# A hybrid decoder layer on one core: the embedding's product by input block, and a fixed order for the last instructions

## The chip, the core and the metric

The kernel runs on one NeuronCore of a Trainium2 chip. Five engines work side by side, each with a queue of its own that it takes strictly in order: TensorE (PE in the profile, with its weight loads as PEld), VectorE (DVE), ScalarE (ACT), GpSimd (POOL) and SyncE (SP), which here only issues transfers. Engines wait for each other through semaphores. Sixteen DMA engines move data between HBM and the on-chip memory SBUF; matmul results go to PSUM, eight banks of 128 x 512 fp32. The metric is the device time of one execution in microseconds, the median of several runs.

## The reference

One decoder layer on 512 tokens of width 1024, in fp32: an FFN, a token mixer, a second FFN, then a gated embedding and a last RMSNorm. Only the last part is touched by the change:

```python
h = h + 0.5 * swiglu(rmsnorm(h, ffn1_norm), ...)
...
h = h + 0.5 * swiglu(rmsnorm(h, ffn2_norm), ...)
gate = sigmoid(rmsnorm(h, ple_norm) @ ple_w_gate + ple_b_gate)
h = h + gate * (p @ ple_w_proj)          # p is (512, 256), ple_w_proj (256, 1024)
return rmsnorm(h, final_norm)
```

The product `p @ ple_w_proj` depends on no other layer's result, so the kernel computes it first of all and stores it in HBM; "the embedding" below is this product.

## The kernel before

**Numbers as pairs.** Every fp32 operand of a product is split into a rounded high part (ACT's cast, `whi`, line 532) and a low part (DVE's difference, `wlo`, line 536). A product is three matmuls: high x high, high x low, low x high. Activations lie feature-major: a tile `h[d]` has 128 features on the partitions and 512 tokens along the free axis; weights are the stationary operand.

**Steps.** The layer up to the second FFN is a list of steps. Each has a load (SP), a split (ACT and DVE), a product (PE) and what comes after the product. Steps 0 and 1 are the embedding, steps 2 to 5 the first block of the FFN in its plain form, from step 6 on a group of seven products of quarter blocks follows for each further block (a Strassen scheme), among them steps with weights that are sums of two loads: POOL issues accumulating loads for these (lines 761 and 764), or DVE adds (`sums`, line 756). Early steps also have the forms of x among their split work: h is scaled and cast (lines 630 and 634), its low parts taken (637), and differences of token halves and feature halves formed (646, 680, 682). Those are the names `split1.1`, `split3.1`, `split4.1`, `split4.2`, `split5.2`, `split5.3` and `split6.2` in the order.

**An order written out by hand.** `run` makes a task of each of these works and then takes them in the order of the text `ENTRY`. `split3.1:4` means the next four instructions of that task, `split3.1` all that is left of it. Within `tc.manual_schedule(engines=ORDERED)` PE, ACT, DVE and SP keep the program's order; POOL is free. Behind that block (the gates and the last norm) a list scheduler orders the instructions by priority and by a model of their times.

**The embedding.** Step q computes four of the eight 128-feature outputs from both input blocks k of p. Step 0's order is k, then pass, then output; step 1's is output first. Step 0 accumulates in three `sm` banks and one `acc` bank, step 1 in three `mm` banks and one `acc` bank. Loads: `p[:, 0]`, step 0's weights in three parts, `p[:, 1]`, then step 1's weights in one transfer and the table of vectors, then the slices of x. `out` (line 1065) copies the four results to SBUF, two on ACT and two on DVE, and `store_embedding` sends them to HBM.

**The tail.** The gates of blocks 0 to 4 are taken for all 512 tokens at a time; those of blocks 5, 6 and 7 by token halves, first half a (tokens 0 to 255) of all three, then half b. `gate` is: a product with r (DVE, 1742), the sigmoid (ACT, 1743), the product with the embedding (DVE, 1744), the sum into h (DVE, 1745), the square (ACT, 1748, or DVE, 1750, for block 7). POOL adds the squares of blocks 0 to 6 into `total` (1769, 1789); `gained` scales h by the last norm's gain. `factors` sums `total` and block 7's square over the features with four small matmuls against a column of ones (1799) and takes the inverse root, for half a by DVE alone (eleven small instructions), for half b with ACT's square root. `rows_out` transposes each chunk of 128 tokens back to rows by PE (1809), two groups of four tiles a chunk, scales one group on ACT (1812) and one on DVE (1814) and stores them (1815). In the program `factors` of half a stands between blocks 6 and 7 of half b, and `rows_out` behind all gates; where they run among the others the scheduler decides.

## Time and profile before

| | us |
|---|---|
| median of three runs | 1072.11 (1071.75 to 1072.2) |
| the profiled execution | 1071.36 |
| its span, first to last instruction | 1069.6 |
| PE busy in the span | 1059.4 |
| DVE, ACT, POOL busy | 781.0, 513.8, 135.5 |

A row of the timeline has the start, the duration, the engine, the line, the operation, the output and inputs by their names in the program, shapes and a count where like instructions are merged, and in brackets how long the engine had been idle and what released it. A row of a table of stretches has each engine's busy time with the count of instructions, the granted clock of TensorE, the mean share of the DMA engines in use and what they moved in GB/s. The chain of waits gives start, length and what the end hung on. The last instruction of the span is not the last computation: the scalings of the last rows begin at 1064.5, and the rest is their way to HBM.

### The profile page before, as it was taken

What the parts mean: (1) busy time and instruction counts of PE and PEld (TensorE: products, weight loads), DVE (VectorE), ACT (ScalarE), POOL (GpSimd) and SP (SyncE); (2) the same over time, 40 slices, a digit from 0 to 9 for tenths busy, and PEclk for the clock granted to TensorE, in tenths of its full rate; (3) what the DMA queues carried; (4) which work ended last, traced back from release to release, by engine and by line L of the source; (5) the groups of instructions that cost most, each with busy time, mean ns of one, the idle gap of its engine ahead of it and who ended that gap; (6) DMA issues with size and microseconds to landing.
All of it is one profiled execution on the core that took longest, in us unless ns stands there. A gap on an engine that the chain in (4) does not pass through costs nothing.

```text
span 1069.6 us, 19076 instructions
## 1 busy us (share of the span) xinstructions
PE 1059.4 (99%) x7926; PEld 993.5 (93%) x7926; DVE 781.0 (73%) x1082; ACT 513.8 (48%) x716; POOL 135.5 (13%) x125
## 2 busy tenths in 40 slices
PE   9999999999999999999999999999999999999997
PEld 8999999999999898887888888999999999999996
DVE  7987676766667686776998756687766677667766
ACT  7644444344444364664753434354444434443554
POOL 0100000000000300034333000001100000000311
PEclk9999999999999999999999999999999999999998
DMA  9987766666523232543431323667766676634412
GB/s 343 307 229 195 190 189 186 162 179 173 138 60 119 71 110 90 154 142 119 154 102 62 105 90 118 214 176 201 197 143 188 162 198 182 187 105 115 142 41 79
DMA packets 50327, 163.70 MB, mean 153 GB/s; under 512 B 5696, under 2 KB 6208, under 8 KB 50240
## 3 DMA queue, kind: packets, MB, share of 16 engines
q1 hardware_dynamic: 40304, 128.86, 35.0%
q0 software_dynamic: 8640, 31.46, 16.9%
q10 hardware_dynamic: 1296, 2.16, 0.7%
q8 instruction: 62, 1.02, 0.4%
q14 instruction: 25, 0.20, 0.1%
HBM read 158.20 MB, written 4.26 MB: 152 GB/s over the span
## 4 chain that ended last, share of the span: by engine, by line
PE 96%; DVE 1%; ACT 1%; DMA 1%; SPq 0%; issue 0%; DVEq 0%; ACTq 0%
PE sm L248 25%; PE mm L746 20%; PE a L746 15%; PE mm L232 7%; PE sm L232 7%; PE mm L248 6%; PE a L232 4%; PE a L248 3%; PE sm L835 2%; PE mm L835 1%; PE a L835 1%; PE sm L301 1%; PE sm L1388 1%; DMA g<-in_p 1%; PE sm L1632 1%; PE sm L1452 0%
## 5 line engine op out<-in xcount | busy, mean ns | idle before, releaser
L532 ACT CAST whi<-raw 128x1024 fp32r<-128x1024 f32 (+1 forms) x140 | 144.4, 1032 | 152.1 <-issue 56.2
L536 DVE TENSOR_TENSOR wlo<-raw,whi 128x1024 fp32r<-128x1024 f32 (+1 forms) x140 | 172.7, 1234 | 60.5 <-ACT whi L532 57.5
L746 PE MATMUL mm<-xfb,whi 128*128 128x256 f32 x960 | 166.1, 276 | 0.0
L248 PE MATMUL sm<-glo,whix 128*128 128x256 f32 (+1 forms) x512 | 151.1, 295 | 0.0
L248 PE MATMUL sm<-ghi,wlox 128*128 128x256 f32 x592 | 150.8, 277 | 0.0
L248 PE MATMUL sm<-ghi,whix 128*128 128x256 f32 (+1 forms) x512 | 150.4, 294 | 0.0
L746 PEld LDWEIGHTS mm<-xfb,whi 128*128 128x128 f32 x960 | 144.5, 188 | 0.0
L746 PE MATMUL mm<-xfb,wlo 128*128 128x256 f32 x480 | 132.5, 276 | 0.0
L248 PEld LDWEIGHTS sm<-ghi,wlox 128*128 128x128 f32 x592 | 111.2, 188 | 6.8
L746 PE MATMUL a<-xfb,whi 128*128 128x256 f32 x640 | 110.8, 276 | 0.0
L746 PEld LDWEIGHTS a<-xfb,whi 128*128 128x128 f32 x640 | 96.3, 188 | 0.0
L248 PEld LDWEIGHTS sm<-ghi,whix 128*128 128x128 f32 x512 | 96.1, 188 | 0.0
L248 PEld LDWEIGHTS sm<-glo,whix 128*128 128x128 f32 x512 | 96.1, 188 | 0.0
L746 PEld LDWEIGHTS mm<-xfb,wlo 128*128 128x128 f32 x480 | 90.1, 188 | 0.0
L536 DVE TENSOR_TENSOR wlox<-rawd,whix 128x1024 fp32r<-128x1024 f32 (+1 forms) x40 | 45.6, 1141 | 60.1 <-ACT whix L532 60.1
L746 PE MATMUL a<-xfb,wlo 128*128 128x256 f32 x320 | 88.3, 276 | 0.0
L536 DVE TENSOR_TENSOR wlo<-rawb,whi 128x1024 fp32r<-128x1024 f32 x52 | 63.6, 1222 | 18.6 <-ACT whi L532 18.5
L895 ACT ACTIVATE g<-g 128x512 f32<-128x512 f32 x40 | 25.3, 632 | 105.4 <-DVE g L893 105.4
L761 POOL DMA_DIRECT2D raw<-in_ffn_gu x20 | 17.3, 865 | 427.1 <-DVE h L951 164.7
L232 PE MATMUL sm<-x,whi 128*128 128x512 f32 x224 | 71.0, 398 | 0.0
L532 ACT CAST whi<-rawb 128x1024 fp32r<-128x1024 f32 x52 | 54.3, 1045 | 27.3 <-DVE rawb L756 17.6
L951 DVE SCALAR_TENSOR_TENSOR h<-sm,h 128x512 f32<-128x512 f32 x96 | 63.5, 683 | 4.4 <-PE sm L248 4.2
(388 smaller groups left out, 2498.0 us busy)
## 6 DMA issues: line engine op xcount, KB each, us to landing
raw<-in_ffn_gu SPq DMA_DIRECT2D x56, 512.0 KB, 6.6
rawd<-in_ffn_down SPq DMA_DIRECT2D x40, 512.0 KB, 4.6
rawb<-in_ffn_gu SPq DMA_DIRECT2D x32, 512.0 KB, 6.1
raw<-in_ffn_gu POOLq DMA_DIRECT2D x30, 512.0 KB, 5.5
raw<-in_w_in SPq DMA_DIRECT2D x28, 512.0 KB, 3.8
s<-in_ffn_gu SPq DMA_DIRECT2D x20, 512.0 KB, 7.7
s<-in_ffn_gu POOLq DMA_DIRECT2D x20, 512.0 KB, 8.9
raw<-in_w_out SPq DMA_DIRECT2D x16, 512.0 KB, 3.4
```

What stands on the lines that cost most here:

```text
L232: nc.tensor.matmul(ps, w, x, start=first and n == 0, stop=last and n == 2, skip_group_check=True)
L248: nc.tensor.matmul(ps[:, tok], wt[:, c], xt[:, tok], start=first and k == i == 0, stop=last and k == len(xs) - 1 and i == len(by_part) - 1 ...
L301: nc.tensor.matmul(ps[:, c : c + 1], part[:, c * P : (c + 1) * P], ones[:, 0:1], start=part is t, stop=part is not t or more is None,)
L532: nc.scalar.copy(self.hi[:, c], self.raw[:, c])
L536: nc.vector.tensor_tensor(self.lo[:, c], self.raw[:, c], self.hi[:, c].bitcast(F32), ALU.subtract)
L746: nc.tensor.matmul(o, wt[:, c], xt, start=fresh and p == m == n == 0, stop=last and n == 2, skip_group_check=True,)
L761: nc.gpsimd.dma_start(w21.raw, self.src[0], accum_op=ALU.add)
L835: nc.tensor.matmul(by_half(ps)[:, s], (whi, whi, wlo)[n][:, c], t[:, s, n % 2], start=not lower and p == i == 0, stop=lower and p == len(s ...
L895: nc.scalar.activation(t, t, AF.Silu)
L951: nc.vector.scalar_tensor_tensor(h[d], ps[d], 0.5, h[d], ALU.mult, ALU.add)
L1388: nc.tensor.matmul(ps, chunk(b_tok[g], c), to_state[g][c], start=True, stop=True)
L1632: nc.tensor.matmul(chunk(ps, c), chunk(v[c][i // 4], i % 4), chunk(ws[i // 4], i % 4), start=True, stop=True,)
```

## The change

Three parts. The embedding is now cut by input block: step k multiplies block k of p with all eight outputs' weights of that block, and adds to eight PSUM banks (three `sm`, three `mm`, two `acc`) that both steps share. Step 0 takes four outputs at a time, pass by pass; step 1 output by output, so that the results are done one after the other, and `out` copies all eight behind step 1. The weights are laid out accordingly by the host. Step 1 loads the first half of its weights, then `p[:, 1]`, then the second half, so one transfer more is issued than before.

```diff
+    def embedding(k):
...
+            if k == 0:
+                nc.sync.dma_start(raw[:, 0], a["p"][:, 0])
+            for c in (first, second, rest) if k == 0 else (whole[0],):
+                nc.sync.dma_start(w.raw[:, c], a["ple_proj"][k][:, c])
+            if k:
+                nc.sync.dma_start(raw[:, 1], a["p"][:, 1])
+                nc.sync.dma_start(w.raw[:, rest], a["ple_proj"][k][:, rest])
                 nc.sync.dma_start(vec, a["vecs"])
...
         def split():
+            raw, hi, lo = (t[:, k] for t in pe)
             w.take()
+            if k == 0:
+                nc.scalar.copy(hi, raw)
+                nc.vector.tensor_copy(w.hi[:, first], w.raw[:, first])
+                nc.scalar.copy(w.hi[:, second], w.raw[:, second])
+            else:
+                nc.scalar.copy(w.hi[:, whole[0]], w.raw[:, whole[0]])
+                nc.scalar.copy(hi, raw)
+            nc.vector.tensor_tensor(lo, raw, hi.bitcast(F32), ALU.subtract)
+            low(whole[0])
+            yield
+            nc.scalar.copy(w.hi[:, rest], w.raw[:, rest])
+            yield
+            low(rest)
...
         def product():
+            if k == 0:
+                emb_ps.extend(acc_ps() if i % 4 == 3 else bank("mm", 3) if i > 3 else sm_ps() for i in range(8))
+            xhi, xlo = pe[1][:, k], pe[2][:, k]
+            order = [(i // 4, n, i) for i in range(8) for n in range(3)]
+            for _, n, i in order if k else sorted(order):
```

The order's text is rewritten up to step 16; from there on it is the same. The part that the prediction speaks of, before and after:

```diff
-product0 split2 load7 product1 after1:1 after0 split3 split3.1:6 split4.1:3 split3.1:1
-split4.1:1 split3.1 split4.1 split5.1:1 load8 after1:1 product2 split4.2:1 split4.2:1 split5.1:1
-after1 split4 split4.2 split6.2:2 load9 product3 split5:1 split5.2:1 split5 split5.1 split6.1
-after4:1 split5.2 split6.2:1 after4 split6.2:1 split5.3 product4 split6 split6.2:1 split6.2
-product5 after4.1 split7 split7.1 load12 product6 split8:1 sums9 after5:1 split8 after6 after5:2
-split9:2 split10.1:1 after5 product7 split10.1:1 split9 load14 product8 split10.1:1 after7
+load6 load6.1 product0 split2 load7 product1 split3 after1:2 split3.1:4 after1:1 split4.1:1
+split3.1:1 after1:1 split4.1:2 split3.1:2 split4.1:1 split3.1 split4.2:1 load8 product2 after1
+split6.2:1 split6.2:1 split5.1:1 split4.2:1 split4 split5.1:1 split4.1 split4.2 load9 product3
+split6.2:2 split5 split5.1 split5.2:1 split6:1 split5.2 split6 split5.3 product4 split6.1 after4
+split6.2 product5 after4.1 split7 split7.1 load12 product6 split8:1 after5:3 sums9 after5
+product7 after6 split8 split10.1:1 split9 load14 split10.1:1 product8 split10.1:1 after7
```

In the tail the program's order is kept from `factors` of half a on, by a second `manual_schedule`; `factors` is cut in two, the sums over `total` (`sums_begin`) and the rest; and for half b `sums_begin` and the first chunk's rows of half a are put between the sigmoid of block 7 and the product with the embedding (`amid`).

```diff
+    def sums_begin(tok):
         ps = sm_ps()
+        for i, c in enumerate(range(tok.start // P, tok.stop // P)):
+            nc.tensor.matmul(
+                ps[:, i : i + 1], total[:, c * P : (c + 1) * P], ones[:, 0:1], start=i == 0, stop=False,
+                skip_group_check=True,
+            )
+        return ps
...
-    for i in range(BY_HALF):
-        if i == BY_HALF - 1:
-            r_a = factors(halves[0], sq_a)
-        sq_b = gate_half(i, halves[1])
-    rows_out(halves[0], r_a)
-    rows_out(halves[1], factors(halves[1], sq_b))
+    for i in range(BY_HALF - 1):
+        gate_half(i, halves[1])
+    with tc.manual_schedule(engines=ORDERED):
+        r_a = factors(sums_begin(halves[0]), halves[0], sq_a)
+        late = {}
+
+        def amid():
+            late.update(ps=sums_begin(halves[1]))
+            rows_out(halves[0], 0, r_a)
+
+        sq_b = gate_half(BY_HALF - 1, halves[1], amid)
+        rows_out(halves[0], 1, r_a)
+        r_b = factors(late["ps"], halves[1], sq_b)
+        for c in (2, 3):
+            rows_out(halves[1], c, r_b)
```

More of the change, by code (lines that the diff above doesn't have):

```diff
@@ L1028, in split @@
         def split():
-            if q:
-                yield from w.split_by_engine()
-                return
-            hi, lo = sb("ghi", (P, 2, T), F32R), sb("glo", (P, 2, T), F32R)
+            raw, hi, lo = (t[:, k] for t in pe)
             w.take()
-            for k in range(2):
-                c = slice(k * T, (k + 1) * T)
-                cast = c if k else halves[1]
-                if k == 0:
-                    nc.scalar.copy(hi[:, 0], raw[:, 0])
-                    nc.vector.tensor_copy(w.hi[:, halves[0]], w.raw[:, halves[0]])
-                nc.scalar.copy(w.hi[:, cast], w.raw[:, cast])
-                if k:
-                    nc.scalar.copy(hi[:, 1], raw[:, 1])
-                for t, r, u in ((hi[:, k], raw[:, k], lo[:, k]), (w.hi[:, c], w.raw[:, c], w.lo[:, c])):
-                    nc.vector.tensor_tensor(u, r, t.bitcast(F32), ALU.subtract)
@@ L1083, in layer_kernel @@
     )
-    steps = [embedding(q) for q in range(2)] + steps
+    steps = [embedding(k) for k in range(2)] + steps
     for d in range(NP):
@@ L1738, in layer_kernel, with gate @@
     r = None
-    def gate(d, ps, tok, engine):
+    def gate(d, ps, tok, engine, amid=lambda: None):
         t = tmp()[:, tok]
@@ L1786, in gate_half @@
         accumulate(ps, units[i], 0, x, parts=(tok,))
[L1787 removed]
+        sq = gate(d, ps, tok, nc.vector, amid)
         if d < ND - 1:
```

122 lines of the change are left out of this document (58 added, 64 removed).

## The prediction, made before the changed kernel ran

> **What bounds the kernel now.** I read the page's busy shares first, then the waits of the tensor engine (PE) over the whole run, then the timelines of the first 50 us and of the last 15 us, engine by engine, because only there does PE stand still. "Idle before, releaser" stands in brackets behind a row.
>
> ```profile
> PE 1059.4 (99%) x7926; PEld 993.5 (93%) x7926; DVE 781.0 (73%) x1082; ACT 513.8 (48%) x716; POOL 135.5 (13%) x125
> PE sm L197 <- DVE tmp L194: 1.7, 1, 1.7
> PE sm L1055 <- ACT ghi L1042: 0.9, 1, 0.9
> PE sm L1799 <- DVE tmp L1750: 0.8, 1, 0.8
> ```
>
> PE is busy for 1059.4 of 1069.6 us and has three waits worth naming. The first is the start itself. The second is inside the embedding, the third in the tail; the change aims at these two. No matmul of the long middle is touched, so whatever lead or lag PE has after the first 50 us it carries to the last gate.
>
> ```profile
> 8.75 0.96 PE L1055 MATMUL sm<-ghi,whi 128*128 128x256 f32 x6 [0.92 <-ACT ghi L1042]
> 17.04 0.62 PE L835 MATMUL sm<-xfa,whi 128*128 128x512 f32 x2
> 17.50 0.39 PE L835 MATMUL sm<-xfa,wlo 128*128 128x256 f32 x2
> 12.23 0.49 DVE L628 TENSOR_SCALAR ghi<-h,vec 128x512 f32<-128x512 f32 x1 [0.23 <-DMA h<-in_x]
> 13.28 2.36 DVE L637 TENSOR_TENSOR xfa<-ghi,xfa 128x1024 fp32r<-128x1024 f32 x2 [0.56 <-ACT xfa L634]
> 15.55 1.22 DVE L536 TENSOR_TENSOR wlo<-raw,whi 128x1024 fp32r<-128x1024 f32 x1
> 15.00:20.00 5.00, 5.00 (x44) 4.88 (x43) 5.00 (x8) 4.18 (x8) 0.00 (x0) 1.00 1.04 406
> 25.00:30.00 5.00, 5.00 (x42) 4.83 (x41) 5.00 (x9) 5.00 (x9) 1.13 (x2) 1.00 1.03 410
> ```
>
> The reader is to see a second limit under the first one. In the two stretches (columns: PE, PEld, DVE, ACT, POOL busy, clock, DMA share, GB/s) the vector engine (DVE) is busy for 5.00 of 5.00 us and the DMA engines are full. DVE's queue hangs on a load: the fourth slice of x lands at 12.23, the forms of x follow at 13.28 to 15.64, and the low half of the first FFN weight ends at 15.55 + 1.22 = 16.77, only 0.73 us before PE reads it at 17.50.
>
> **The change part by part: the start.** The embedding keeps its 96 matmuls. PE runs one in 0.113 us (two each at 17.50 and its neighbours), so step 0 would run from 4.8 to about 10.4 without a break and step 1 to about 15.8, against 17.04 now: up to 1.3 us, of which 0.92 is the named wait. Step 1's second half of p lands later than now, one 256 KB load further back; at the 406 GB/s of the first stretch above that is 0.65 us, about 8.7 instead of 8.05 (2.65 + 5.40, the row of the chain of waits below), and its cast and low half (0.6 and 0.7, like other tiles of 128x512) are done by 10.1, in time.
>
> ```profile
> 2.65 5.40 DMA g<-in_p
> ```
>
> What stalls next is FFN product 2. Its first PSUM bank is now freed later: the order puts the cast of weight 3 ahead of the copies of outputs 0 and 1, and its second weight row is no earlier than x allows.
>
> ```profile
> 14.09 1.05 ACT L532 CAST whi<-raw 128x1024 fp32r<-128x1024 f32 x1
> 15.51 1.07 ACT L1065 COPY embt<-sm 128x512 f32<-128x512 f32 x2
> 16.47 1.07 ACT L532 CAST whi<-raw 128x1024 fp32r<-128x1024 f32 x1
> 26.89 1.21 DVE L536 TENSOR_TENSOR wlo<-raw,whi 128x1024 fp32r<-128x1024 f32 x1
> 28.43 0.39 PE L835 MATMUL sm<-xfb,wlo 128*128 128x256 f32 x2
> ```
>
> On ScalarE (ACT) the new order is cast 2 at 14.1, cast 3 at 15.05, then the copies at 16.0, so bank 0 is free at about 16.6 and product 2 starts there: 0.3 us of lead is left of 1.3. Product 3 now needs the bank of output 4, whose copy on ACT comes behind five casts and forms of x (my addition of ACT's pitches gives 22.0 to 22.6, where product 3 starts at 17.04 + 48 x 0.113 = 22.5 now): the lead is gone. Product 4 needs the low half that DVE ends at 28.10 now. Counting DVE's instructions ahead of it (0.60 us a pitch for 512 columns, 1.14 for 1024) the new order has the same 10.2 us between the low halves of products 2 and 4, with the two copies and the T1 forms moved ahead and two other low halves behind: 28.1 again, against a read at 28.43. So PE reaches product 6 within -0.3 to +0.25 us of now. The 0.92 us were covered by DVE and by loads all along.
>
> The next place decides. Product 8 (the fourth weight block of the first Strassen group) is begun at 44.8, and its low half is first read at 45.04.
>
> ```profile
> 38.35 1.05 ACT L532 CAST whi<-raw 128x1024 fp32r<-128x1024 f32 x1 [1.83 <-DMA raw<-in_ffn_gu]
> 40.82 1.03 ACT L532 CAST whi<-rawb 128x1024 fp32r<-128x1024 f32 x1
> 41.76 0.57 ACT L344 COPY rall<-sm 128x512 f32<-128x512 f32 x1
> 41.56 1.23 DVE L756 TENSOR_TENSOR rawb<-rawb,s 128x1024 f32<-128x1024 f32 x1 [0.49 <-DMA s<-in_ffn_gu]
> 42.70 0.68 DVE L856 TENSOR_TENSOR g<-sm,rall 128x512 f32<-128x512 f32 x1
> 43.30 1.22 DVE L536 TENSOR_TENSOR wlo<-rawb,whi 128x1024 fp32r<-128x1024 f32 x1
> 45.04 0.28 PE L746 MATMUL mm<-xfb,wlo 128*128 128x256 f32 x1
> ```
>
> Now DVE does the weight sum (L756) while it waits for ACT's copy of r, then one half of the gate (L856), then the low half for product 8, which ends at 44.52: 0.5 us to spare. The new order is both halves of the gate ("after5:3"), then the sum ("sums9"), and the low half behind all of it. The gate cannot start before the copy of r ends at 41.76 + 0.57 = 42.33, and that hangs on the accumulating load that lands at 38.35. So: gate halves 42.37 and 42.97, sum 43.57, low half 44.71 to 45.93. PE reads it at 45.97 instead of 45.04: **+0.93 us**, and DVE idles for about a microsecond before the gate. A lead or lag of up to 0.7 us that PE brings to this place makes no difference to it. Bounds: if the accumulating load lands 1 us earlier the term is between -0.3 and +0.25; each tenth later adds a tenth.
>
> **The tail.** The last half gate is that of block 7, tokens 256 to 511.
>
> ```profile
> 1056.58 0.60 PE L1809 MATMUL mm<-ident,h 128*128 128x128 f32 x4
> 1057.72 0.72 POOL L1789 TENSOR_TENSOR ssum<-ssum,tmp 128x256 f32<-128x256 f32 x1 [1.80 <-ACT tmp L1748]
> 1058.50 0.38 PE L1799 MATMUL sm<-ones,ssum 128*128 128x1 f32 x2
> 1058.58 0.42 DVE L1742 TENSOR_TENSOR tmp<-sm,rall 128x256 f32<-128x256 f32 x1
> 1059.87 0.42 DVE L1744 TENSOR_TENSOR tmp<-tmp,emb 128x256 f32<-128x256 f32 x1 [0.22 <-ACT tmp L1743]
> 1060.21 0.74 DVE L1814 TENSOR_SCALAR o<-a,rlast 128x512 f32<-128x512 f32 x1
> 1060.87 0.41 DVE L1745 TENSOR_TENSOR h<-h,tmp 128x256 f32<-128x256 f32 x1
> 1060.47 0.55 PE L1809 MATMUL mm<-ident,h 128*128 128x128 f32 x3
> 1061.80 0.38 PE L1799 MATMUL sm<-ones,tmp 128*128 128x1 f32 x2 [0.78 <-DVE tmp L1750]
> 1062.05 0.36 PE L1799 MATMUL sm<-ones,ssum 128*128 128x1 f32 x2
> 1062.49 0.41 PE L1809 MATMUL mm<-ident,h 128*128 128x128 f32 x2
> 1062.67 0.16 DVE L267 TENSOR_SCALAR nv<-sm 128x2 f32<-128x2 f32 x1 [0.53 <-PE sm L1799]
> 1063.00:1063.50 0.50, 0.00 (x0) 0.00 (x0) 0.34 (x3) 0.06 (x1) 0.00 (x0) 0.70 0.13 45
> ```
>
> Now PE transposes half a's rows from 1056.58, while GpSimd (POOL) still adds block 6's square to the total (until 1058.44). An output scaling (L1814) stands in DVE's queue between the product with the embedding and the sum (L1744, L1745). The change takes that one away from there, worth 0.66 us, and one pair of sum matmuls behind the square, worth 0.24. But it puts the total's sums on PE ahead of the transposes, and PE is in order: queued behind them are all 16 transposes of half a, and for those wait ACT's and DVE's scalings. They start when POOL is done, 1058.50 + 2 x 0.23 = 1058.96. Two groups of four (0.43 each, 0.17 to the end) are ready at 1060.0, so DVE's scaling, which the fixed order puts ahead of L1744, runs 1060.03, L1744 1060.69, L1745 1061.15, the square 1061.60 to 1062.03, the gain 1062.06, the scaling of chunk 1 1062.33, and L267 1062.99 against 1062.67: **+0.32 us**. The sums behind the square are done by 1062.64 and do not bind any more. Without the wait for POOL the same additions give 1061.91, a gain of 0.76; with the half gate's own work delayed by as much again it would be +0.7. I take +0.32.
>
> The sixteen transposes of half b now all come after the square's sums, at 1062.5 to 1064.3, where all but the last two were done by 1061.0 (1060.47 + 0.55). The granted clock falls to 0.50 at about 1063.2 (0.70 in the half microsecond from 1063.0). No row shows a transpose at 0.50: its price lies between nothing and a doubled pitch, with which the last group is ready at 1065.6 where DVE is free for it at 1064.94, +0.65. I take +0.3, between the ends. **Sum: 0.93 + 0.32 + 0.3 = +1.55 us.**
>
> **Rivals.** *The loads come earlier.* The DMA share is only 0.45 in the sixth microsecond, so a hole could close when the loads are cut anew; for it speaks that ACT's wait of 1.83 us at 38.35 is one for a load, against it that the bytes and their order behind x stay.
>
> ```profile
> 5.00:6.00 1.00, 1.00 (x11) 1.00 (x10) 0.84 (x2) 0.24 (x2) 0.00 (x0) 1.00 0.45 160
> 9.00:10.00 1.00, 1.00 (x10) 1.00 (x10) 1.00 (x2) 0.71 (x1) 0.00 (x0) 1.00 1.05 394
> ```
>
> It decides from 0.9 us earlier at 38.35, where product 8 stops waiting. With 1.2 us the start gives -0.35, and with the tail's +0.62 the result is +0.27, not slower: 1072.4. With 2 us, and POOL early as well, -1.3 - 0.76 = -2.1, which is where faster begins.
>
> *POOL's add is done in time* (block 6's gate a microsecond sooner in the queues): the tail gains 0.76, 0.93 - 0.76 = +0.17, 1072.3. Against it: nothing of block 6 is edited.
>
> *The loads come later.* One load more is issued ahead of x (0.43 to 0.47 us apiece on the queue), and p's and x's start depend on it. All arrivals shift by it: +1.55 + 0.45 to 0.9 = +2.0 to +2.5, 1074.4. For it: the hole at 5 us shows DMA engines without work while requests are queued.
>
> *The clock falls before the last transposes begin.* All sixteen at a doubled pitch (0.217) take 3.5 us from 1062.5, and the last group is ready at 1066.2, 1.2 us behind DVE: 0.93 + 0.32 + 1.2 = +2.45, 1074.6. [...]
>
> **How the numbers follow.** The profiled execution took 1071.36 us, 1.76 more than its span of 1069.6, and lies 0.75 below the median 1072.11 of the three runs; I add the sum to the median: 1072.11 + 1.55 = **1073.7**. Chances: the forecast 0.50 (own range 1072.6 to 1074.8), loads earlier 0.17, POOL in time 0.08, loads later 0.13, clock early 0.12. 0.2% is 2.14 us, about what a measurement of this kernel can tell from no change; it begins at 1074.25 above and 1069.97 below. From the forecast's share a third lies above 1074.25 when its two unknown prices come out high; with most of the last two cases that is 0.32 slower. Faster needs the far end of the loads' case: 0.12, which is more than its working gives, since an order of the first steps may hide DVE better than my addition of pitches does. The same: 0.56. The range, 1070.7 to 1075.7, reaches from the loads' case with a kept lead to the clock's case with a later load.
>
> **What would show it.** Right: no wait of PE for the cast of p at step 1; a wait of about 0.7 us before the low half of product 8, with DVE idle ahead of the first gate; the first FFN product 0.3 us earlier and the spread of r within 0.3 us of now; PE waiting for POOL before the tail's transposes; L267 bound by DVE's own queue and not by PE. Wrong: x or the accumulating load landing more than half a microsecond away from now; the total's sums served at once; PE's lead of about 1 us kept at 60 us.

## The result, and the profile after

The changed kernel takes 1073.76 us (median of 20 executions), the kernel before 1071.68 us in 20 executions of the same session: +2.08 us, ratio 1.0019, interval 1.0013 to 1.0025, just inside the 0.2% that the prediction took as no change. One execution of the twenty took 2174.73 us; the median of the other nineteen is 1073.67 us, +1.99. The profiled execution took 1073.61 us with a span of 1071.9, against 1071.36 and 1069.6 before.

The waits of the tensor engine in the first 70 us and in the tail of the changed kernel, as in the view shown of before (total, count, longest in us), and in the last row one of its weight loads (PEld):

```profile
PE sm L1819 <- POOL ssum L1796: 1.8, 1, 1.8
PE sm L198 <- DVE tmp L195: 1.7, 1, 1.7
PE sm L1827 <- DVE tmp L1757: 1.2, 1, 1.2
PE sm L836 <- ACT embt L1073: 0.5, 1, 0.5
PE mm L747 <- DVE wlo L537: 0.3, 1, 0.3
PEld mm L836 <- ACT rawd L1073: 0.3, 1, 0.3
```

The 0.9 us wait for p's cast is gone. Three of PE's are new: for the copy of output 0 (L836, `sm`), for product 8's low half (L747) and for POOL's add (L1819). The one for block 7's square (L1827) has grown from 0.8 to 1.2 us. Product 3's first weight load waits for the copy of output 4 (L836, `mm`), as the prediction has it. The timeline of the changed kernel around product 8 and, behind it, where its last group of products ends:

```profile
12.52 0.48 DVE L629 TENSOR_SCALAR ghi<-h,vec 128x512 f32<-128x512 f32 x1 [0.66 <-DMA h<-in_x]
16.91 0.73 PE L836 MATMUL sm<-xfa,whi 128*128 128x512 f32 x2 [0.46 <-ACT embt L1073]
42.37 1.29 DVE L857 TENSOR_TENSOR g<-sm,rall 128x512 f32<-128x512 f32 x2 [0.87 <-ACT rall L345]
43.57 1.22 DVE L757 TENSOR_TENSOR rawb<-rawb,s 128x1024 f32<-128x1024 f32 x1
44.70 1.22 DVE L537 TENSOR_TENSOR wlo<-rawb,whi 128x1024 fp32r<-128x1024 f32 x1
45.28 0.39 PE L747 MATMUL mm<-xfb,whi 128*128 128x256 f32 x2
45.98 0.38 PE L747 MATMUL mm<-xfb,wlo 128*128 128x256 f32 x1 [0.30 <-DVE wlo L537]
46.20 0.40 PE L747 MATMUL mm<-xfb,whi 128*128 128x256 f32 x2
57.15 0.39 PE L249 MATMUL sm<-ghi,whi 128*128 128x512 f32 x1
```

The gate, the sum and the low half come at 42.37, 43.57 and 44.70, and PE reads the low half at 45.98: each within 0.01 us of the forecast. The 0.30 in brackets counts from the end of the matmul before; from start to start, 113 ns being usual, PE comes 0.47 us late. What was not forecast stands in the chain of waits (start, length, what), first of before, then of after:

```profile
47.70 2.72 PE a L746 x24
50.42 2.72 PE mm L746 x24
```

```profile
48.84 2.83 PE a L747 x24
51.66 2.83 PE mm L747 x24
```

The same 24 matmuls take 2.83 instead of 2.72 us, 118 ns apiece instead of 113, from the wait until 57.15. Over these 11 us that is half a microsecond more.

The tail of the changed kernel:

```profile
1057.91 0.28 PE L249 MATMUL sm<-x,wlo 128*128 128x256 f32 x1
1059.97 0.61 PE L1819 MATMUL sm<-ones,ssum 128*128 128x1 f32 x4 [1.78 <-POOL ssum L1796]
1060.44 0.64 PE L1805 MATMUL mm<-ident,h 128*128 128x128 f32 x4
1060.91 0.60 PE L1805 MATMUL a<-ident,h 128*128 128x128 f32 x4
1061.55 0.75 DVE L1813 TENSOR_SCALAR o<-a,rlast 128x512 f32<-128x512 f32 x1 [1.09 <-PE a L1805]
1062.22 0.42 DVE L1751 TENSOR_TENSOR tmp<-tmp,emb 128x256 f32<-128x256 f32 x1
1064.52 0.15 DVE L268 TENSOR_SCALAR nv<-sm 128x2 f32<-128x2 f32 x1
1065.79 1.41 DVE L1813 TENSOR_SCALAR o<-mm,rlast 128x512 f32<-128x512 f32 x2
```

PE stands still for 1.78 us until POOL's add is done, the transposes follow, DVE waits 1.09 us for them with L1751 to L1765 queued behind, and L268 (L267 before) comes straight out of DVE's own queue, with no idle time ahead of it.

The stretches of the changed kernel's end (same columns as before) show a full clock until the last transpose:

```profile
1064.00:1065.00 1.00, 1.00 (x11) 1.00 (x12) 0.73 (x3) 0.20 (x1) 0.00 (x0) 1.00 0.77 285
1065.00:1066.00 1.00, 1.00 (x10) 0.78 (x8) 0.79 (x5) 0.22 (x1) 0.00 (x0) 1.00 0.55 205
```

### The profile page after: what moved, and what is told of

It reads as the page before. It is cut to its first block, busy times and chain, and to the rows that moved or that the text cites. A ratio compares the mean times of both kernels' runs of the same rounds, so it can differ in the third digit from the quotient of the medians.

```text
span 1071.9 us, 19073 instructions
## 1 busy us (share of the span) xinstructions
PE 1060.5 (99%) x7926; PEld 994.4 (93%) x7926; DVE 781.7 (73%) x1083; ACT 514.9 (48%) x717; POOL 135.7 (13%) x125
## 3 DMA queue, kind: packets, MB, share of 16 engines
HBM read 158.20 MB, written 4.26 MB: 152 GB/s over the span
## 4 chain that ended last, share of the span: by engine, by line
PE 93%; DVE 2%; DMA 2%; ACT 1%; issue 1%; SPq 0%; POOLq 0%; POOL 0%; DVEq 0%
PE sm L249 24%; PE mm L747 20%; PE a L747 15%; PE mm L233 7%; PE sm L233 7%; PE mm L249 6%; PE a L233 4%; PE a L249 3%; PE sm L836 1%; DMA emb_dram<-rawd 1%; DMA raw<-in_ffn_gu 1%; DMA h<-in_x 1%; PE sm L302 1%; PE sm L1394 1%; PE mm L836 1%
## 5 line engine op out<-in xcount | busy, mean ns | idle before, releaser
L533 ACT CAST whi<-raw 128x1024 fp32r<-128x1024 f32 (+2 forms) x139 | 143.1, 1031 | 153.3 <-issue 56.4
L537 DVE TENSOR_TENSOR wlo<-raw,whi 128x1024 fp32r<-128x1024 f32 (+2 forms) x139 | 171.5, 1235 | 59.6 <-ACT whi L533 58.9
L747 PE MATMUL mm<-xfb,whi 128*128 128x256 f32 x960 | 166.3, 276 | 0.0
L249 PE MATMUL sm<-glo,whix 128*128 128x256 f32 (+1 forms) x512 | 151.1, 295 | 0.0
L249 PE MATMUL sm<-ghi,wlox 128*128 128x256 f32 x592 | 150.8, 277 | 0.0
L249 PE MATMUL sm<-ghi,whix 128*128 128x256 f32 (+1 forms) x512 | 150.4, 294 | 0.0
L747 PEld LDWEIGHTS mm<-xfb,whi 128*128 128x128 f32 x960 | 144.6, 188 | 0.0
L747 PE MATMUL mm<-xfb,wlo 128*128 128x256 f32 x480 | 132.7, 276 | 0.3 <-DVE wlo L537 0.3
L249 PEld LDWEIGHTS sm<-ghi,wlox 128*128 128x128 f32 x592 | 111.2, 188 | 6.8
L747 PE MATMUL a<-xfb,whi 128*128 128x256 f32 x640 | 110.9, 276 | 0.0
L747 PEld LDWEIGHTS a<-xfb,whi 128*128 128x128 f32 x640 | 96.4, 188 | 0.0
L249 PEld LDWEIGHTS sm<-glo,whix 128*128 128x128 f32 x512 | 96.1, 188 | 0.0
L249 PEld LDWEIGHTS sm<-ghi,whix 128*128 128x128 f32 x512 | 96.1, 188 | 0.0
L747 PEld LDWEIGHTS mm<-xfb,wlo 128*128 128x128 f32 x480 | 90.2, 188 | 0.5 <-DVE wlo L537 0.5
L747 PE MATMUL a<-xfb,wlo 128*128 128x256 f32 x320 | 88.4, 276 | 0.0
L533 ACT CAST whi<-rawb 128x1024 fp32r<-128x1024 f32 x52 | 54.3, 1044 | 25.8 <-DVE rawb L757 17.6
```

The costliest lines, as they stand in the source:

```text
L249: nc.tensor.matmul(ps[:, tok], wt[:, c], xt[:, tok], start=first and k == i == 0, stop=last and k == len(xs) - 1 and i == len(by_part) - 1 ...
L533: nc.scalar.copy(self.hi[:, c], self.raw[:, c])
L537: nc.vector.tensor_tensor(self.lo[:, c], self.raw[:, c], self.hi[:, c].bitcast(F32), ALU.subtract)
L747: nc.tensor.matmul(o, wt[:, c], xt, start=fresh and p == m == n == 0, stop=last and n == 2, skip_group_check=True,)
```

## The experiments

Each ran 11 times beside runs of the kernel before; the interval of each ratio is about 0.0009 (1 us) to either side, so single terms are read from the traces. The table has for each profiled execution the start of product 6, of step 12 (L249's first row), of the last row of the last gate's product ("last acc."), of the row `nv` (L267 or L268, where DVE takes the last sums of squares from PE), the end of the last scaling, and the span.

| kernel | median against before (ratio) | product 6 | step 12 | last acc. | nv | scaled | span |
|---|---|---|---|---|---|---|---|
| before | | 39.37 | 55.70 | 1056.46 | 1062.67 | 1065.37 | 1069.6 |
| after | +2.08 (1.0019) | 39.84 | 57.15 | 1057.91 | 1064.52 | 1067.20 | 1071.9 |
| start_alone | +1.26 (1.0012) | 40.30 | 58.01 | 1058.55 | 1064.76 | 1067.46 | 1072.2 |
| tail_alone | +0.22 (1.0004) | 39.80 | 56.22 | 1056.70 | 1064.23 | 1066.91 | 1071.2 |
| old_order_from_product6 | +0.92 (1.0009) | 39.97 | 56.30 | 1056.78 | 1063.70 | 1067.87 | 1071.3 |
| rows_before_sums | +0.76 (1.0007) | 39.64 | 56.63 | 1057.11 | 1062.65 | 1066.92 | 1070.3 |
| wait_alone | +0.83 (1.0008) | 39.66 | 56.93 | 1057.77 | 1063.99 | 1066.70 | 1071.0 |
| before_mended_tail | -0.57 (0.9995) | 39.80 | 56.12 | 1056.90 | 1062.41 | 1065.10 | 1069.4 |
| both_mended | -0.26 (0.9995) | 39.15 | 56.24 | 1056.91 | 1062.41 | 1065.11 | 1069.8 |
| both_mended_2 | -0.72 (0.9993) | 39.75 | 56.39 | 1057.13 | 1062.63 | 1065.34 | 1070.0 |
| tail_alone_pe_kept_busy | +0.49 (1.0004) | 39.91 | 56.35 | 1057.08 | 1063.67 | 1066.36 | 1070.6 |
| after_two_wide_matmuls | +2.01 (1.0018) | 39.36 | 57.71 | 1058.19 | 1065.23 | 1069.29 | 1072.7 |
| before_one_load_more | +0.23 (1.0004) | 39.63 | 55.96 | 1056.64 | 1062.86 | 1065.55 | 1070.3 |
| both_mended_2_seven_loads_more | -1.00 (0.9990) | 39.03 | 55.36 | 1056.02 | 1061.53 | 1064.23 | 1068.5 |

### The parts by themselves

**start_alone**: the changed embedding and order with before's tail.

> The embedding by input block and the rewritten order up to step 16, with the tail of before. Reading of the two traces (theory A): everything up to the last gate stays as in the changed kernel, so PE is 1.45 us behind before at the end of the last accumulation, and the tail's row L268 (nv) comes 1.45 us behind before's 1062.67: +1.4 to +1.5 us in the median, +0.14%. Of this +0.47 are brought to product 6, +0.47 is the longer wait before product 8's low half, and +0.5 the slower pitch of the matmuls behind that wait. Rival B (my prediction's sum): the wait is all that counts, +0.93. Rival C: the late output stores (0.45 us) belong to the start as well: +1.9.

Measured +1.26 us. The sum of theory A is about right and its parts are not. Product 6 begins at 39.37 to 39.91 in the six executions with before's start (before, tail_alone, wait_alone, before_mended_tail, tail_alone_pe_kept_busy, before_one_load_more) and at 39.36 to 40.30 in the five with the changed start (after, start_alone, old_order_from_product6, rows_before_sums, after_two_wide_matmuls): means 39.70 and 39.82. So most of the 0.47 us is the profiled execution of before being an early one. Rival C is right about the end: 1072.2 - 1067.46 = 4.7 us from the last scaling to the end of the span, with before's tail.

**tail_alone**: before's embedding and order with the changed tail.

> The fixed order of the tail with the total's sums ahead, on the embedding and the order of before. Theory A (the traces): L267 comes 0.40 us later than before's 1062.67 because PE waits for POOL's add and DVE for PE's transposes, and the last landing another 0.45 later: +0.4 to +0.85 us. Rival (the prediction's first estimate): +0.32 and no more. Rival (the change as meant: POOL's add is in time): -0.76 us. If the 0.45 us between the last scaling and the last landing show here as well (4.7 instead of 4.2 us from the last scaling to the end of the span), they belong to the tail's order; if not, to chance.

Measured +0.22 us; the end has before's 4.25 us (1071.16 - 1066.91), so the 0.45 us belong to the start's part, not to the tail or to chance. From the last accumulation to `nv` it is 1064.23 - 1056.70 = 7.53 us here, 6.61 in after, 6.21 in before. The reason is the clock; PE's rows and the stretch in this execution:

```profile
1058.74 0.67 PE L1813 MATMUL sm<-ones,ssum 128*128 128x1 f32 x4 [1.76 <-POOL ssum L1790]
1059.27 1.10 PE L1799 MATMUL mm<-ident,h 128*128 128x128 f32 x4
1060.16 1.06 PE L1799 MATMUL a<-ident,h 128*128 128x128 f32 x4
```

```profile
1060.00:1061.00 1.00, 1.00 (x6) 1.00 (x5) 0.00 (x0) 0.60 (x1) 0.00 (x0) 0.50 0.00 0
```

A group of four transposes takes 0.89 us (1059.27 to 1060.16) where after's takes 0.47 (1060.44 to 1060.91), and DVE waits for them the longer. Four of the eleven executions, with a mean granted clock of 0.997 to 0.998, took 1072.4 to 1073.2 us; the seven at 0.999 took 1071.3 to 1072.1 (medians 1072.86 and 1071.62).

**wait_alone**: before with after's text of the order from product 6 on.

```diff
-product6 split8:1 sums9 after5:1 split8 after6 after5:2 split9:2 split10.1:1 after5 product7
+product6 split8:1 after5:3 sums9 after5 product7 after6 split8 split10.1:1 split9
...
```

> Before's embedding, loads and tail; only the text of the order from product 6 to product 14 is that of the changed kernel, so that both halves of the gate and the sum stand ahead of product 8's low half. Theory A (the wait, and in some executions a slower pitch behind it): PE reads the low half at about 45.97 instead of 45.04, +0.93 us; behind it either 113 ns a matmul as in the run with the rows ahead of the sums (46.54 us on), then +0.9 us in all, or 118 ns up to 57 us as in the changed kernel and in the run with the start alone, then +1.4 us. Rival B (the wait is covered, because the old start feeds this place in another way): 0. Rival C (the slow pitch comes from the new embedding's phase, not from the wait): +0.9 in every execution and 113 ns.

Measured +0.83 us. Rival B falls; PE's rows of this execution:

```profile
46.16 0.38 PE L746 MATMUL mm<-xfb,wlo 128*128 128x256 f32 x1 [0.61 <-DVE wlo L536]
46.73 0.39 PE L746 MATMUL mm<-xfb,whi 128*128 128x256 f32 x2
```

From product 6 to step 12 it takes 17.27 us (56.93 - 39.66) against 16.32 to 16.44 in six executions with the old order there: +0.9 (the seventh, both_mended, is spoken of below). Behind the wait the matmuls here keep 113 ns. This run does not exclude rival C. Against it speaks that 118 ns also came with before's start, at other places (in before_mended_tail until 18.2 us, in tail_alone_pe_kept_busy from 28.8 to 31.8 us), and behind product 8's wait in only two of the four kernels with the changed one.

**old_order_from_product6** is the reverse: the changed kernel with before's text from product 6 on.

> The changed kernel, with the text of the order from product 6 to product 14 put back to that of before: the sum for step 9 stands first, one half of the gate behind it, then the low half for product 8. Theory A: no wait before product 8's low half, and with it no slower pitch behind it; PE keeps the 0.47 us that it is late at product 6, so 0.47 + 0.5 = 0.97 us are gained against the changed kernel, +1.1 us against before. Rival B: the slower pitch has nothing to do with the wait (it belongs to the embedding or to the code's place): gain 0.47 only, +1.6 against before, and pairs of 256-wide matmuls still begin 0.235 us apart from 46 to 57 us. Rival C: the slow pitch stays gone but the old order stalls elsewhere, because it was made for a PE that comes 0.47 us earlier: no gain at product 14.

Measured +0.92 against before, 1.16 below the changed kernel, from product 6 to step 12 16.33 us, and pairs of matmuls at 0.39 from 40 us on: theory A. Together the two runs settle that the order from product 6 on makes the start slower, and the one long wait of PE that comes and goes with it is product 8's low half: 17.31 us from product 6 to step 12 in after, 16.99 to 17.71 in the other kernels with this order (the run with two matmuls more set aside), +0.67 to +1.4.

**rows_before_sums** exchanges two lines of the tail.

```diff
         def amid():
-            late.update(ps=sums_begin(halves[1]))
             rows_out(halves[0], 0, r_a)
+            late.update(ps=sums_begin(halves[1]))
```

> The changed kernel, with two lines of the tail exchanged: the transposes of the first chunk of half a now stand ahead of the total's sums of half b in PE's queue. Theory A (PE's wait for POOL holds up the transposes, and DVE's queue behind them): the transposes run at about 1058 instead of 1060.44, DVE's scaling of the first chunk starts at once behind the product with r, and L268 comes 0.9 to 1.0 us earlier than the changed kernel's 1064.52: +1.1 us against before. Rival B: the wait for POOL only moves (the transposes of the second chunk then wait for it, and DVE's second scaling with them): a gain below 0.3 us. Rival C: another engine's wait ends last (the sigmoid, ACT's scalings): between the two.

Measured +0.76, 1.3 below the changed kernel. `nv` follows the last accumulation after 5.54 us instead of 6.61, theory A's 0.9 to 1.0 and a little more:

```profile
1057.23 0.60 PE L1805 MATMUL mm<-ident,h 128*128 128x128 f32 x4
1059.13 0.61 PE L1819 MATMUL sm<-ones,ssum 128*128 128x1 f32 x4 [0.87 <-POOL ssum L1796]
1059.54 0.74 DVE L1813 TENSOR_SCALAR o<-a,rlast 128x512 f32<-128x512 f32 x1
1066.17 0.75 DVE L1813 TENSOR_SCALAR o<-mm,rlast 128x512 f32<-128x512 f32 x1 [0.95 <-PE mm L1805]
```

DVE's scaling starts straight behind the product with r. In this execution the clock fell at 1061.6, and the last row shows the price: DVE waits for half b's transposes, and the last scaling ends 4.27 us behind `nv` instead of 2.70.

### Versions that mend a part

**before_mended_tail**: before's start; the exchange above, and fourteen of half b's sixteen transposes ahead of the last sums. The cut shows the second of these; `turn` and `scaled` are the transposes and the scalings of `rows_out`.

```diff
...
+        early = {}
+        for c in (2, 3):
+            for q in range(2):
+                early[c, q] = mm_ps()
+                turn(c, q, early[c, q], range(4 - q))
         r_b = factors(late["ps"], halves[1], sq_b)
         for c in (2, 3):
-            rows_out(halves[1], c, r_b)
+            turn(c, 1, early[c, 1], (3,))
+        for c in (2, 3):
+            scaled(halves[1], c, r_b, (early[c, 0], early[c, 1]))
```

> Before's embedding and order with a mended tail: the first chunk's transposes and scalings of half a ahead of the total's sums, and the fourteen transposes of half b whose tiles are done ahead of the last sums, with two behind. Theory A (what the tail costs is PE's queue behind POOL, and the transposes of half b at whatever clock is granted): L267 0.6 to 0.7 us earlier than before's 1062.67, as in the run with the rows ahead of the sums (its distance from the last accumulation was 5.54 instead of 6.21 us), and the last scaling 2.7 us behind it: -0.5 to -0.7 us against before, -0.8 against the run of the tail alone. Rival B (the scaling of the second chunk in DVE's queue takes the gain): -0.2 or less. Rival C (the clock falls whatever the order and the last sums and two transposes pay for it): 0 to +0.4.

Measured -0.57; the ratio's interval, 0.9986 to 1.0003, reaches no change. In the traces it is 5.51 us from the last accumulation to `nv` against 6.21 in before, and 2.69 from there to the last scaling: the idea of a fixed tail was sound, its order was not.

**both_mended**: the changed embedding with an order of its own for the first six steps, before's order from product 6, the mended tail.

```diff
-product1 split3 after1:2 split3.1:4 after1:1 split4.1:1
-split3.1:1 after1:1 split4.1:2 split3.1:2 split4.1:1 split3.1 split4.2:1 load8 product2 after1
-split6.2:1 split6.2:1 split5.1:1 split4.2:1 split4 split5.1:1 split4.1 split4.2 load9 product3
+product1 after1:2 split3 split3.1:4 after1:1 split4.1:1
+split3.1:1 after1:2 split4.1:2 split3.1:2 split4.1:1 split3.1 split4.2:1 load8 product2 after1
+split5.1:1 split4.2:1 split4 split6.2:1 split6.2:1 split5.1:1 split4.1 split4.2 load9 product3
...
```

> The embedding by input block with an order of its own for the first six steps: the copies of outputs 0 and 1 ahead of the cast of weight 3, output 4's copy in ACT's idle time at 19.5, DVE's low half of weight 4 ahead of the forms for T1, ACT's last row sums ahead of step 6's cast; from product 6 on the order of before; the mended tail. Theory A (the 0.47 us at product 6 are the order's, not the embedding's): product 2 starts at 16.0 instead of 16.91, its low half is read at about 17.2, product 4's at 28.1, product 6 begins 0.0 to 0.3 us ahead of before's 39.37, and the median is 0.1 to 0.3 us below that of before's start with the mended tail: -0.6 to -0.9 us against before. Rival B (x's later landing, 0.3 us, is what DVE hands on, whatever the order): product 6 at 39.6 or later and the median 0.2 to 0.5 us above that of before's start with the mended tail. Rival C (a new wait, at the spread of r or at product 7): slower still.

Product 6 came at 39.15, as theory A has it, and the median is 0.3 us above the run before it, as rival B has it, but not for rival B's reason. Up to the end of the last scaling the two executions agree within 0.01 us (1065.11 and 1065.10), and the 0.43 us by which this span is longer lie behind it: they are the end that the changed start has with either tail, explained below. The lead itself was lost at product 7:

```profile
40.74 1.22 DVE L537 TENSOR_TENSOR wlo<-raw,whi 128x1024 fp32r<-128x1024 f32 x1
42.01 0.19 PEld L747 LDWEIGHTS mm<-xfb,wlo 128*128 128x128 f32 x1
42.11 0.29 PE L747 MATMUL mm<-xfb,wlo 128*128 128x256 f32 x1
42.23 0.40 PE L747 MATMUL mm<-xfb,whi 128*128 128x256 f32 x2
45.06 0.39 PE L747 MATMUL mm<-xfb,wlo 128*128 128x256 f32 x1
```

The low half ends at 41.96 and PE loads it at 42.01, 125 ns behind the load before it where 113 is usual: some 12 ns behind its turn (15 in the expectation below, read from 42.004). That is no wait that any view lists, but from here to 56.9 us a matmul takes 118 ns, and product 6 to step 12 takes 17.09 us instead of 16.33.

**both_mended_2** moves two low halves forward.

```diff
-split5.3 split6.2 product5 after4.1 split7 split7.1 load12
-product6 split8:1 sums9 after5:1 split8 after6 after5:2 split9:2 split10.1:1 after5
+split5.3 product5 after4.1 split7 split6.2 split7.1 load12
+product6 split8:1 sums9 split8 after5:1 after6 split9:1 after5:2 split9 split10.1:1 after5
```

> As the run with both parts mended, with DVE's order changed once more: the low half for product 7 ahead of the last two low parts of T1, and the low half for product 8 directly behind the sum, ahead of both gate halves. In the run before it PE came to product 7's low half 15 ns too early (42.004 us) and the matmuls behind it ran at 118 instead of 113 ns until 57 us. Theory A (a weight that comes just in time is enough to start the slow pitch): no wait at products 7 and 8, 113 ns from 39 us on in the profile, PE 0.2 us ahead of before at product 6 and still at product 14, median 0.3 to 0.6 us below the run with both mended (1071.26): 1070.7 to 1071.0, -0.5 to -0.9 against before. Rival B (the slow pitch comes by chance, whatever DVE's order): median as the run with both mended. Rival C (another low half is late instead, product 9's or 10's): the same or above.

Measured -0.72, where theory A has it; but the two medians lie 0.46 us apart with 1 us to either side of each, which does not exclude rival B. In the profiled execution product 7 has no wait any more, product 8 a short one (its low half ends at 45.55, PE reads it at 45.60, 0.18 us late), and 113 ns hold from 40 us on all the same. The lead at product 6 is missing from this execution (39.75: here the matmuls ran at 118 ns until 20.6 us and again from 28.6 to 34.5 us) and is there again in the last run (39.03).

**tail_alone_pe_kept_busy** adds twelve matmuls that nothing reads to the tail alone.

```diff
         def amid():
+            accumulate(spare, units[2], 0, x[:2])
             late.update(ps=sums_begin(halves[1]))
             rows_out(halves[0], 0, r_a)
...
         rows_out(halves[0], 1, r_a)
+        for _ in range(2):
+            accumulate(spare, units[2], 0, x[:1])
```

> The tail alone (before's embedding and order), with twelve 512-wide matmuls more that nothing reads: six while PE waits for POOL's add, six behind the transposes of half a's second chunk, while PE waits for the square. Theory A (the fixed order's price is the clock: all sixteen transposes of half b and, where the clock falls already behind the last accumulation, half a's too run at 0.50; this came in four of eleven executions of the tail alone, at 1072.4 to 1073.2 against 1071.3 to 1072.1): the clock stays at 1.00 until the last transpose, no execution above 1072.3, median 1071.6 to 1071.9. Rival B (the spread is the start's, by the pitch of the matmuls): the same two groups as in the tail alone. Rival C (the added matmuls hold the tail's own up): all executions 0.3 us or more slower than the lower group of the tail alone.

The clock did as theory A said (0.999 or 1.0 in ten of eleven executions), the time did not: median 1072.25, four executions above 1072.3. In the profiled execution `nv` comes 6.59 us behind the last accumulation, as in after (6.61): the order's own price of 0.4 us stays, only the clock's part goes. Why the seven good executions of the tail alone had a median equal to before's, without these 0.4 us, no trace shows; the medians of eleven don't bear more.

**after_two_wide_matmuls**: two 512-wide matmuls more at the start of product 9.

> The changed kernel with two 512-wide matmuls more, which nothing reads, at the start of product 9, 2.8 us behind the wait before product 8's low half. Theory A (the slow pitch behind a wait lasts until 512-wide matmuls follow each other, as where it ended in the changed kernel at 57.15 us): behind product 8's wait 118 ns a matmul, from product 9 on 113 ns; the two cost 0.46 us and save about 0.3 (some 70 matmuls at 4.5 ns), so +0.1 to +0.2 against the changed kernel. Rival B (the pitch is set by something else there: loads in flight, DVE, ACT): 118 ns until 57 us as in the changed kernel, and +0.46 against it. Where the wait does not start the slow pitch at all, as in two of four such waits so far, the run does not tell.

The profiled execution had its wait (0.62 us before product 8's low half) and 113 ns behind it, so this run doesn't tell.

### The end of the kernel

From the last scaling to the end of the span it was 4.25 to 4.27 us with before's embedding and 4.69 to 4.71 with the new one, wherever the clock held to the last transpose. The instruction records of SP's last steps name the semaphores it waits for (start in us, semaphores), before left, after right:

```
before                               after
1066.053 last store, semaphore 110   1067.893 last store, semaphore 101
1066.503 waits for 118, 117          1068.342 waits for 118, 117
1066.567 waits for 101, 116          1070.578 waits for 101, 116
1066.628 waits for 103, 115          1070.640 waits for 103, 115
...                                  ...
1068.736 waits for 110, 102          1071.008 waits for 110, 102
```

In both traces the transfers of SP and ACT take eight semaphores in turn (101, 103, 105 to 110; 296 transfers in before, 297 in after), and at the end SP waits for these one after the other, in the same order. In before the last store holds the last of the eight and lands at 1068.72; the other waits have passed by then. In after it holds the first and lands at 1070.56, and the other seven waits, 0.06 us each, come behind that (1070.640 to 1071.008).

**before_one_load_more**: one load of the gate's weights as two transfers, nothing else. **both_mended_2_seven_loads_more**: seven such, so that the turn is complete again.

```diff
-        accumulate(ps, weights(a["ple_gate"][d], D), 0, x, parts=halves)
+        accumulate(ps, weights(a["ple_gate"][d], D, parts=2 if d == 2 else 1), 0, x, parts=halves)
...
```

> Before, with the load of the gate weights of block 2 issued as two transfers of half the size; nothing else differs on any engine. Over the profiled executions so far the time from the last scaling to the end of the span is 4.25 to 4.27 us with before's embedding and 4.69 to 4.71 with the new one, wherever the clock stayed at 1.00 until the last scaling, whatever the tail. The new embedding issues one transfer more. The trace shows that the transfers of SP and ACT take eight semaphores in turn (101, 103, 105 to 110), that SP at the very end waits for them one after the other in this fixed order, and that the last store holds the eighth in before (296 transfers) and the first in the changed kernel (297): there all the other waits come behind the last landing. Theory A (the end's 0.44 us are the turn of the semaphores): 4.7 us from the last scaling to the end, +0.4 us in the median (0.1 to 0.7 with the spread of eleven executions). Rival B (they belong to the embedding in another way): 4.26 us, and no difference in the median.

> The second version with both parts mended, with the loads of the gate weights of blocks 1 to 7 issued as two transfers each, so that the last store holds the eighth semaphore again. Theory A: 4.26 instead of 4.70 us from the last scaling to the end of the span, 0.44 us below the run before it (-0.72 against before): -1.1 to -1.2 us against before, 1070.4 to 1070.7. Rival B: as the run before it, 4.70 us. Rival C (seven transfers more cost something on SP's queue or split the DMA engines' work badly in the last 70 us): above the run before it.

The last scaling and the first line of the answer, with the span, of the first and of the second:

```profile
core 0 of [0], span 1070.3 us
1064.14 1.41 DVE L1816 TENSOR_SCALAR o<-mm,rlast 128x512 f32<-128x512 f32 x2
```

```profile
core 0 of [0], span 1068.5 us
1062.82 1.41 DVE L1813 TENSOR_SCALAR o<-mm,rlast 128x512 f32<-128x512 f32 x2
```

4.7 us (1070.26 - 1065.55) and 4.3 us (1068.49 - 1064.23): the place moved as forecast in both, and the cause rests on these traces. The medians alone would not show it: +0.23, with no change inside the interval (0.9995 to 1.0013), and -1.00 against -0.72 without the seven loads. The -1.00 is 1070.55 us, interval 0.9981 to 0.9999: of the versions tried, the only one whose interval lies wholly below before, by 0.1 to 2.0 us.

## Why the prediction was right, and where it was not

The forecast was 1072.11 + 1.55 = 1073.7, the result 1073.76. The places and most of the mechanisms were right; that the two numbers agree to 0.1 us is luck. Two errors cancel: the base, a median of three executions, was 0.43 above the median of twenty (1071.68), and the sum lacked 0.5 us (+1.55 for +2.08). Point by point:

- **Product 8's low half, +0.93: right in place and mechanism.** It is read at 45.98, forecast 45.97. So close a hit is chance: in the five executions with this order it came at 45.84 to 46.84, and PE stood still for 0.47 to 0.78 us. By itself the order cost +0.83 in the median. The forecast did not have the slower pitch that may follow such a wait, up to 0.5 us more: it came in two of five such executions (after, start_alone) and not in wait_alone, rows_before_sums and after_two_wide_matmuls. What decides, no run shows.
- **The embedding itself, nothing: right.** "The 0.92 us were covered by DVE and by loads all along": product 2 is 0.13 us earlier (forecast 0.3, though the start at 16.6 that it worked out would be 0.44), and product 6 is on average 0.1 us later, within the -0.3 to +0.25 forecast; the +0.47 of the one profile lies within the scatter of executions. "All along" goes too far, though: with another order of the first steps product 6 came at 39.15 (both_mended) and 39.03 (both_mended_2_seven_loads_more), some 0.6 us ahead of the mean with before's start, 39.70 (and at 39.75 in both_mended_2, with the slower pace for much of the way). In the changed kernel's profile the only waits of PE and its loads between the embedding and product 6 are those for the copies of outputs 0 and 4 on ACT: its order held PE up, not DVE and the loads under any order. The last slice of x reached DVE at 12.52 instead of 12.23, but at 11.87 to 12.66 over all executions, whichever the start: the rivals on earlier and later loads fall.
- **The tail, +0.32: right, +0.40.** PE waits for POOL, DVE for PE, and L268 hangs on DVE's queue. The exchange of two lines gave back 1.07 us, more than the 0.76 that the prediction had without the wait. "POOL in time" falls (1.78 us of wait).
- **The clock, +0.3 between 0 and +0.65: right on average, wrong in shape.** In the profile it cost nothing. Of the nineteen executions the thirteen with a mean clock of 0.998 or more have a median of 1073.63, the six below it 1074.36: +0.73 in a third of them, 0.23 on the mean. The upper bound was too low: in the tail alone the two groups lie 1.2 us apart. The step failed where it let the clock reach half b's last transposes alone; it also reaches half a's (0.50 from 1059.15 us in tail_alone, from 1060.0 in old_order_from_product6, from 1061.3 in after_two_wide_matmuls). That the clock falls early is thus not a rival to the forecast but a part of it that some executions pay. That the six longer executions of the changed kernel pay it at this place is inferred from their mean clock; none of them was profiled.
- **The end, 0: wrong, +0.44.** The prediction priced the added transfer as a delay of the loads behind it ("0.43 to 0.47 us apiece"), which cost nothing, and took the way from the last scaling to the end as fixed. This term is missing from the sum. That 1.55 + 0.44 = 1.99 is the measured difference of the nineteen executions is chance again, since the order's term alone measured +0.67 to +1.4.

The parts don't add up exactly: the start alone +1.26 (of which 0.83 the order and 0.44 the end) and the tail alone +0.22 make 1.48, not 2.08. The difference is inside what three medians of eleven executions leave open.

## What to carry to other kernels

Where one engine (here DVE) is full, read its queue up to the next product whose operand it makes: a step that the bound engine can do while it waits for another (the sum, during the copy of r) must not be put behind that wait, and an operand that is ready a few tenths of a microsecond ahead leaves room for the scatter of executions (half a microsecond here, at product 6). A fixed order also fixes its mistakes: here sums that had to wait for POOL, put ahead of transposes that were ready, cost 1.07 us until the two lines were exchanged. Before a small difference is put down to a step, look at the same point in several executions; and when a transfer is added, look at the waits at the very end as well.

## What the runs showed that was not expected

- **A second pace of the matmuls at full clock.** In the fourteen profiled executions PE runs at 118 ns a matmul of 256 columns instead of 113 in eleven stretches, at a granted clock of 1.00, and each of them ends behind a pair of 512-wide matmuls: six begin in the embedding and end in product 2 (17.6 to 20.7 us; in after at 20.4), two lie at 28 to 35 us, and three follow a weight half that came late (by 0.47 us in after, 0.78 in start_alone, some 12 ns in both_mended) and last for 95 to 115 such matmuls, to step 12's first or second such pair (57.15 us in after). Three of the five long waits for product 8's low half and the one of 0.18 us in both_mended_2 did not bring it. What starts it stays open: the run made for it, after_two_wide_matmuls, did not have it there.
- **The clock behind PE's wait for POOL.** In before the profile records a clock of 1.00 from 5.07 to 1063.20 us and of 0.50 behind that, in after of 1.00 from 4.71 to 1069.67 us. Four of the fourteen executions have PE's wait of 1.75 to 1.78 us for POOL's add. Behind its end the clock fell to 0.50 after 0.4 us in tail_alone (1058.74 and 1059.15), 1.2 us in old_order_from_product6 (1058.81 and 1060.0) and 1.1 us in after_two_wide_matmuls (1060.23 and 1061.3); in after it stayed at 1.00 for another 9.7 us (1059.97 and 1069.67). With matmuls put into the wait (tail_alone_pe_kept_busy, where 0.39 us of it were left) it was 1.00 in every stretch from 1056 to 1066. The time at 0.50 was 3.41 us in tail_alone (to 1062.56) and 6.8 us in old_order_from_product6 (to 1066.8). One-column matmuls and transposes (fp32, MATMUL rows in the profile) were all that PE did in the tail of after from 1059.97 on, at a clock of 1.00, and in tail_alone between 1058.74 and the clock's return at 1062.56; in rows_before_sums, with the same kinds of work, the clock fell at 1061.6 and was still 0.50 between 1066 and 1067. A stretch ahead of a fall and two without one lie close to each other: in before PE stood still for 1.1 of the last 3.41 us (1059.79 to 1063.20), beside 0.7 us of one-column matmuls and 1.6 of transposes; in after for 1.0 us, beside 0.5 and 1.9, in each of the stretches 1059.43 to 1062.84 and 1062.84 to 1066.26. What sets the moment of the fall, no run shows.
- **The number of transfers moves the end.** One transfer of SP more, in the embedding or in the gate's loads, made the way from the last scaling to the end 0.44 us longer (4.69 to 4.71 us instead of 4.25 to 4.27), and seven further ones took it back (4.26 us), as the turn of the eight semaphores in the traces of before and after has it.
